# A two-layer decoder trunk with input and parameters laid out by feature, and its first four tiles made k-tile by k-tile

## The chip, the cores and the metric

The kernel runs on one core of a Trainium2 chip. The metric is the device time of one execution in microseconds. Before, the median of three runs is 1343.31 us.

## What is computed

A trunk of two layers on 512 tokens of width 1024, everything in float32. Each layer multiplies the normed input with one matrix of 3344 columns; its parts go to an attention with 8 heads and to a Mamba-2 state-space block (16 heads, a causal convolution of width 4 over x, B and C). Both outputs go through one output product into the residual, and a SwiGLU with a hidden width of 2816 follows.

```python
def hybrid_mixer(h, w_in, ...):
    proj = h @ w_in
    q, k, v, z, xbc, dt = jnp.split(proj, [Q_END, K_END, V_END, Z_END, XBC_END], axis=-1)
    attn = dilated_attention(q, k, v)                      # after a partial rotary on q and k
    xbc = jax.nn.silu(causal_depthwise_conv(xbc, conv_w, conv_b))
    dt = jax.nn.softplus(dt + dt_bias)
    y = ssd_chunked(xs, dt, -jnp.exp(a_log), bm, cm) + d_skip[:, None] * xs
    y = rmsnorm(y * jax.nn.silu(z), ssm_norm)              # in two groups
    return jnp.concatenate([attn, y], axis=-1) @ w_out

for layer in range(DEPTH):
    h = h + hybrid_mixer(rmsnorm(h, norm_mix[layer]), w_in[layer], ...)
    h = h + swiglu(rmsnorm(h, norm_ffn[layer]), w_gate[layer], w_up[layer], w_down[layer])
return rmsnorm(h, final_norm)
```

## The kernel before

The residual lies feature-major on the chip: eight tiles hT of 128 features by 512 tokens. A float32 product is made of three products in float32r: both operands are split into a high part and a low rest (xh, xl and whi, wlo), and hi x hi, hi x lo and lo x hi are added in one accumulator. One output tile of 128 columns over 8 k-tiles is thus 24 products of 512 columns (`block`, line 506). dt's tile needs only 16, since its 16 columns hold high and low parts side by side. The norm's scale (one number per token) is put on the accumulator as it is read out (`scaled`, line 744), so the products don't wait for it; but every read of an accumulator does wait for the norm's row.

The program is a list of operations, each with an engine, a duration and a priority (a due time, set by `at`). A list schedule (`Plan.schedule`, line 217) runs a model of the engines and takes, on each engine, the ready operation of the lowest priority number; the order that comes out is fixed, and every engine runs its instructions in that order. SyncE's DMA queue goes by priority alone and stops where a load waits for its buffer. PSUM has 3 buffers for accumulators (acc), 2 held longer (hold) and 3 for transposes and small things (tr); there are 2 buffers for raw weights of up to 2048 columns each and 3 each for whi and wlo; 56 buffers (G) hold 128 x 512 tiles.

The head of the program, which the change touches:

- Lines 446 to 457: ident (the identity for transposes), mrow (norm weights of the mixer as rows) and the first half of the input, token-major, are loaded. mrow is transposed to pmix (line 465).
- Line 575: the weights of the first two tiles, 128 columns each. The chunk for the third and fourth tile (line 765) waits for a raw buffer, and the loads behind it in the queue wait with it.
- Lines 577 to 588: each input tile is transposed on TensorE (4 transposes a tile, 32 in all) into PSUM; `split_x` takes xh (ScalarE) and xl (VectorE) from there, and a copy makes hT; its squares are summed for the norm.
- Lines 591 to 618: the other parameters arrive as rows (prow, crow) and are transposed to prm and cvp; lines 643 to 657 spread d_skip over features with a product (dskr, dsk). The constant array cst (line 605) feeds the selectors sele, lt, rt and, with the positions, the rotary tables (lines 661 to 735).
- Lines 763 to 774: the first two tiles of layer 0 are made in halves, since the second half of the input comes later; then tiles three and four. `conv` (line 753) reads a finished accumulator (tile cu, with the norm's row), and does one ScalarE step, three VectorE steps and a Silu. Behind these four tiles come dt's (line 779) and the tiles of x and z.

`Norm.spread` (line 557) makes the row: eight small products sum the squares over features (tr<-ones,sq), VectorE scales them (var), GpSimd raises them to -0.5 (rcol, line 554), four transposes and a ScalarE copy spread them to all partitions (rstd).

Of the kernel before, what the change touches and what calls it, by code (L numbers as in the profile page):

```python
# [13 lines left out]
I32 = mybir.dt.int32  # L14
# [5 lines left out]
P = 128  # L20
# [29 lines left out]
# columns of the constant array  # L50
# [3 lines left out]
# columns of the transposed parameter rows  # L54
PC_MIX, PC_FFN, PC_FIN, PC_SSM, PC_DTB, PC_ALOG, PC_DSK, PC_W = 0, 16, 32, 40, 64, 66, 68, 70
# [103 lines left out]
class VTile:  # L159
    """A tile that gets its place when its first operation is emitted."""  # L160
# [22 lines left out]
class Plan:  # L183
# [139 lines left out]
def hybrid_trunk(  # L323
    ctx: ExitStack,
    tc: tile.TileContext,
    x, positions, norm_mix, w_in, conv_w, conv_b, dt_bias, a_log, d_skip, ssm_norm,
    w_out, norm_ffn, w_gate, w_up, w_down, final_norm, consts, out,
# [43 lines left out]
    def at(t):  # L371
        plan.t = t

    # ---- operations
# [52 lines left out]
    def mms(outs, prods, each, prio=None):  # L427
        """prods: (out, lhsT, rhs, start, stop), or (out, in, identity) for a transpose."""
# [17 lines left out]
    at(-40.0)  # L446
    ident = C([P, P], "ident")
# [3 lines left out]
    xt = {}  # L451

    def load_x(hf):
        for i in range(NT):
            xt[i, hf] = G("x")
            load(xt[i, hf], x[0, i * P:(i + 1) * P, hf * S:(hf + 1) * S], 256)
    load_x(0)
# [5 lines left out]
    pmix = C([P, 16], "pmix")  # L463
    t = tr()
    tposes(t, [(t[:, 0:16], mrow, ident[0:16, 0:16])])
    copy("dve", pmix, t[:, 0:16])

# [1 line left out]
    # A chunk is one load; its pieces, 128 columns each, are split into float32r parts hi + lo.  # L469
# [36 lines left out]
    def block(segs, lead=LEAD, t=None, total=None, done=0):  # L506
        """One output tile: segs of (weight piece, operands, first and last k-tile)."""
        t = acc() if t is None else t
        total = total or sum(k1 - k0 for _, _, k0, k1 in segs)
        for pid, xl, k0, k1 in segs:  # L510
            at(clock[0] - lead)
            if whl[pid][4] is None:
                split_w(pid, "pool" if pid == 1 else "dve")
                whl[pid].append(k0)
# [16 lines left out]
    hT = [C([P, S], f"hT{k}") for k in range(KD)]  # L531

    class Norm:
        """Sum of squares over feature tiles, then 1/rms per token, as a row on all partitions."""
# [39 lines left out]
    # the first operands, out of the token-major input  # L574
    p_first = rows(w_in[0], 0, KD, XBC_COL + 1024, P) + rows(w_in[0], 0, KD, XBC_COL + 1024 + P, P)
    xs_next, norm_next = [], Norm(KD)
    for k in range(KD):
        if k == 4:
            at(-30.0)
            load_x(1)  # L580
        at(-20.0 + k)
        t = hold() if k < 2 else acc() if k == 2 else tr()
        tposes(t, [(t[:, i * P:(i + 1) * P], xt[i, k // 4][:, (k % 4) * P:(k % 4 + 1) * P], ident) for i in range(NT)])
        xs_next.append(split_x(t, pmix[:, k:k + 1]))
        at(-9.0 + k)
        copy("dve" if k % 2 else "act", hT[k], t)
        at(0.4 * k)
        norm_next.square(hT[k])
# [603 lines left out]
```

## Time and profile before

| | |
|---|---|
| runs, us | 1338.26, 1343.31, 1344.51 |
| median, us | 1343.31 |
| span of the profiled execution, us | 1336.7 |
| TensorE busy, us | 1310.3 (98%) |
| VectorE busy, us | 789.0 (59%) |
| ScalarE busy, us | 608.4 (46%) |
| GpSimd busy, us | 143.2 (11%) |
| DMA | 115.46 MB, 86 GB/s in the mean |

The span runs from the first to the last instruction of one execution under the profiler; a time of that execution apart from its span is not among the figures. PE is TensorE, PEld its weight loads, DVE VectorE, ACT ScalarE, POOL GpSimd, SP SyncE with the DMA queue. A matmul's busy time is modelled and overlaps the next one's, so the distance between two starts is what a product takes, not its duration. L436 and the like are lines of helpers, so the tile names tell what an instruction does.

### The profile page before, as it was taken

What the parts mean: (1) busy time and instruction counts of PE and PEld (TensorE: products, weight loads), DVE (VectorE), ACT (ScalarE), POOL (GpSimd) and SP (SyncE); (2) the same over time, 40 slices, a digit from 0 to 9 for tenths busy, and PEclk for the clock granted to TensorE, in tenths of its full rate; (3) what the DMA queues carried; (4) which work ended last, traced back from release to release, by engine and by line L of the source; (5) the groups of instructions that cost most, each with busy time, mean ns of one, the idle gap of its engine ahead of it and who ended that gap; (6) DMA issues with size and microseconds to landing.
All of it is one profiled execution on the core that took longest, in us unless ns stands there. A gap on an engine that the chain in (4) does not pass through costs nothing.

```text
span 1336.7 us, 15604 instructions
## 1 busy us (share of the span) xinstructions
PE 1310.3 (98%) x6118; PEld 1053.4 (79%) x6118; DVE 789.0 (59%) x1312; ACT 608.4 (46%) x956; POOL 143.2 (11%) x111
## 2 busy tenths in 40 slices
PE   7999998999999999999999999999999999999997
PEld 6778777678888888888888777767788888888876
DVE  5996689766444334444469687887744433344443
ACT  5878755654332223223347686466532222232233
POOL 1002456000000000000000235520000000000000
PEclk9999999999999999999999999999999999999999
DMA  5221111222222232222322221111332323332141
GB/s 176 95 95 64 63 63 32 64 63 95 95 95 75 96 129 95 95 87 96 117 84 76 67 92 64 38 58 38 91 115 84 97 74 102 111 123 67 61 160 63
DMA packets 111744, 115.46 MB, mean 86 GB/s; under 512 B 4492, under 2 KB 102072, under 8 KB 111672
## 3 DMA queue, kind: packets, MB, share of 16 engines
q1 hardware_dynamic: 111672, 114.47, 26.7%
q8 instruction: 48, 0.79, 0.3%
q14 instruction: 24, 0.20, 0.0%
HBM read 112.37 MB, written 2.10 MB: 86 GB/s over the span
## 4 chain that ended last, share of the span: by engine, by line
PE 89%; DVE 5%; ACT 2%; POOL 2%; issue 1%; DMA 1%; SPq 0%; POOLq 0%; DVEq 0%; ACTq 0%
PE acc L436 79%; PE tr L436 4%; PE tr L434 3%; PE hold L436 3%; DVE qs L384 1%; DVE xbc L395 1%; DVE wlo L384 1%; ACT whi L421 1%; POOL qr L384 0%; DMA raw<-in_w_down_dram 0%; POOL xbc L384 0%; DMA x<-in_x_dram 0%; DVE qs L949 0%; DVE sa L390 0%; DVE sa L1007 0%
## 5 line engine op out<-in xcount | busy, mean ns | idle before, releaser
L436 PE MATMUL acc<-xh,whi 128*128 128x512 f32 x1584 | 628.2, 397 | 1.4 <-ACT whi L421 1.1
L436 PE MATMUL acc<-xl,whi 128*128 128x512 f32 x1584 | 618.6, 391 | 0.0
L436 PE MATMUL acc<-xh,wlo 128*128 128x512 f32 x1568 | 613.2, 391 | 0.3 <-DVE wlo L384 0.3
L421 ACT CAST whi<-raw 128x1024 fp32r<-128x1024 f32 (+4 forms) x260 | 224.0, 867 | 490.3 <-PE acc L436 455.9
L436 PEld LDWEIGHTS acc<-xh,whi 128*128 128x128 f32 x1584 | 298.3, 188 | 66.8 <-issue 5.5
L436 PEld LDWEIGHTS acc<-xh,wlo 128*128 128x128 f32 x1568 | 295.0, 188 | 64.2 <-DVE wlo L384 1.5
L436 PEld LDWEIGHTS acc<-xl,whi 128*128 128x128 f32 x1584 | 298.5, 188 | 59.2 <-issue 0.5
L384 DVE TENSOR_TENSOR wlo<-raw,whi 128x1024 fp32r<-128x1024 f32 (+4 forms) x251 | 258.7, 1035 | 63.0 <-ACT whi L421 62.3
L384 DVE TENSOR_TENSOR ga<-acc,rstd 128x512 f32<-128x512 f32 x44 | 30.4, 692 | 182.4 <-PE acc L436 181.8
L384 DVE TENSOR_TENSOR hT<-hT,acc 128x512 f32<-128x512 f32 x80 | 54.8, 685 | 109.0 <-PE acc L436 108.3
L423 ACT ACT_TABLE_LOAD x54 | 69.3, 1283 | 6.4 <-DVE pmix L401 3.5
L555 POOL TENSOR_TENSOR rcol<-var,nhalf 128x4 f32<-128x4 f32 x8 | 8.7, 1091 | 558.3 <-DVE var L390 558.3
L395 DVE SCALAR_TENSOR_TENSOR xbc<-cu,cvp,xbc 128x511 f32<-128x511 f32 (+2 forms) x72 | 58.5, 816 | 3.2 <-ACT xbc L423 2.3
L384 DVE TENSOR_TENSOR up<-acc,rstd 128x512 f32<-128x512 f32 x44 | 30.3, 688 | 45.0 <-PE acc L436 44.9
L421 ACT CAST xh<-ga 128x512 fp32r<-128x512 f32 x44 | 27.4, 623 | 58.4 <-DVE ga L384 58.4
L423 ACT ACTIVATE sa<-sa,mx 128x512 f32<-128x512 f32 (+3 forms) x64 | 36.0, 562 | 36.6 <-DVE mx L1007 35.1
L1151 POOL TENSOR_TENSOR fr<-fvar,nhalf 128x1 f32<-128x1 f32 x4 | 2.2, 547 | 356.9 <-DVE fvar L390 356.9
L384 DVE TENSOR_TENSOR xl<-ga,xh 128x512 fp32r<-128x512 f32 x44 | 30.3, 688 | 15.1 <-ACT xh L421 15.1
L1007 DVE CUSTOM_DVE_ANT_0 sa<-tr,cst 128x512 f32<-128x512 f32 (+3 forms) x64 | 30.5, 477 | 10.3 <-PE tr L436 10.1
L384 DVE TENSOR_TENSOR ga<-ga,up 128x512 f32<-128x512 f32 x44 | 30.3, 689 | 3.7 <-ACT ga L423 1.4
L384 DVE TENSOR_TENSOR ee<-ee,cbm 128x512 f32<-128x512 f32 x32 | 26.0, 817 | 6.9 <-ACT ee L423 6.9
L384 POOL TENSOR_TENSOR xbc<-xbc,er 128x384 f32<-128x384 f32 x16 | 20.1, 1258 | 83.3 <-DVE er L384 43.1
(203 smaller groups left out, 1184.9 us busy)
## 6 DMA issues: line engine op xcount, KB each, us to landing
raw<-in_w_in_dram SPq DMA_DIRECT2D x25, 1024.0 KB, 5.0
raw<-in_w_gate_dram SPq DMA_DIRECT2D x20, 1024.0 KB, 5.2
raw<-in_w_up_dram SPq DMA_DIRECT2D x20, 1024.0 KB, 5.3
raw<-in_w_down_dram SPq DMA_DIRECT2D x16, 768.0 KB, 4.3
raw<-in_w_out_dram SPq DMA_DIRECT2D x8, 1024.0 KB, 4.9
raw<-in_w_down_dram SPq DMA_DIRECT2D x12, 640.0 KB, 4.4
raw<-in_w_out_dram SPq DMA_DIRECT2D x8, 512.0 KB, 5.0
x<-in_x_dram SPq DMA_DIRECT2D x8, 256.0 KB, 4.6
```

What stands on the lines that cost most here:

```text
L384: lambda: ENG[eng].tensor_tensor(R(o), R(a), R(b), alu))
L395: lambda: nc.vector.scalar_tensor_tensor(R(o), R(a), R(s), R(b), op0, op1))
L421: nc.scalar.copy(R(o), R(a))
L423: nc.scalar.activation(R(o), R(a), func, **kw)
L434: nc.tensor.transpose(R(p[0]), R(p[1]), R(p[2]))
L436: nc.tensor.matmul(R(p[0]), R(p[1]), R(p[2]), start=p[3], stop=p[4])
L555: lambda: nc.gpsimd.tensor_tensor(R(self.r), R(v), R(nhalf), ALU.pow))
L1007: nc.vector.tensor_tensor_reduce(R(sa[:, 0:nk]), R(t[:, 0:nk]), R(cst[:, C_MASK + S - nk:C_MASK + S]), 1.0, 3e38, ALU.add, ALU.min, R(m))
L1151: lambda r=r, v=v: nc.gpsimd.tensor_tensor(R(r), R(v), R(nhalf[:, 0:1]), ALU.pow))
```

## The change

The host hands over the input transposed (xT, feature by token), the positions by partition, and one array `columns` with all small parameters already as columns on 128 partitions (d_skip spread over features, dt_bias and a_log on the rows of the four quadrants). The loads put them in place: hT directly from xT, pmix, prm and posi from the arrays. All transposes of the input and of parameter rows are gone, as are mrow, prow, crow, cvp, posr and the product for d_skip. pmix is kept for the first split; every later use of the norm weights reads prm.

The first four output tiles of layer 0 are no longer made one after another with weights cut by `split_w`. Each k-tile's weights for all four, 128 x 512, are a load of their own (raw0, in G buffers); hT and weights of one k-tile are loaded in turn. For each k, xh, xl, wh and wl are made, and 12 products go to four accumulators that stay open through all 8 k-tiles: two acc and two hold.

```diff
-    load(ident, consts[:, C_ID:C_ID + P], 64)
-    mrow = C([16, P], "mrow")
-    load(mrow, norm_mix.rearrange("l (k p) -> (l k) p", p=P), 8)
...
+    pmix = C([P, 16], "pmix")
+    load(pmix, columns[:, PC_MIX:PC_MIX + 16], 8)
+    hT = [C([P, S], f"hT{k}") for k in range(KD)]
+    raw0 = []
+    for k in range(KD):
+        load(hT[k], xT[k * P:(k + 1) * P, :], 256)
+        raw0.append(G("w0"))
+        load(raw0[k], w_in[0, k * P:(k + 1) * P, XBC_COL + 1024:XBC_COL + 1024 + S], 256)
...
-    p_first = rows(w_in[0], 0, KD, XBC_COL + 1024, P) + rows(w_in[0], 0, KD, XBC_COL + 1024 + P, P)
+    first = [acc(), acc(), hold(), hold()]
     for k in range(KD):
-        if k == 4:
-            at(-30.0)
-            load_x(1)
         at(-20.0 + k)
-        t = hold() if k < 2 else acc() if k == 2 else tr()
-        tposes(t, [(t[:, i * P:(i + 1) * P], xt[i, k // 4][:, (k % 4) * P:(k % 4 + 1) * P], ident) for i in range(NT)])
-        xs_next.append(split_x(t, pmix[:, k:k + 1]))
-        at(-9.0 + k)
-        copy("dve" if k % 2 else "act", hT[k], t)
-        at(0.4 * k)
+        xs_next.append(split_x(hT[k], pmix[:, k:k + 1]))
+        wh, wl = split_x(raw0[k], None)
+        for j, t in enumerate(first):
+            js = slice(j * P, (j + 1) * P)
+            xh, xl = xs_next[k]
+            mms([t], [(t, wh[:, js], xh, k == 0, False), (t, wh[:, js], xl, False, False),
+                      (t, wl[:, js], xh, False, k == KD - 1)], 0.2165, clock[0])
+            clock[0] += 3 * 0.2165
+        at(-12.0 + k)
         norm_next.square(hT[k])
...
     at(-12.0)
-    prow = C([PC_W, P], "prow")
...
+    prm = C([P, PC_W], "prm")
+    load(prm, columns, 94)
+    posi = C([P, NT], "posi", I32)
+    load(posi, positions, 2)
+    ident = C([P, P], "ident")
+    load(ident, consts[:, C_ID:C_ID + P], 64)
     cst = C([P, C_W], "cst")
     load(cst, consts, 400)
...
-            first = [block([(pb[i], xs, 0, 4)], 24.0, None, KD) for i in range(2)]
-            for i in range(2):
-                xbc[8 + i] = conv(block([(pb[i], xs, 4, KD)], 24.0, first[i], KD, 4), 8 + i)
+            for i in range(4):
+                xbc[8 + i] = conv(first[i], 8 + i)
...
-                    stt(xbc[jj], xbc[jj], dsk[:, l * 8 + jj:l * 8 + jj + 1], yd[u2], ALU.mult, ALU.add)
+                    stt(xbc[jj], xbc[jj], pcol(PC_DSK + l * 8 + jj), yd[u2], ALU.mult, ALU.add)
```

With the four tiles made ahead of `layer`, the due time at which layer 0 starts (T0), and with it that of the norm's row and of the four convolutions, is 20.8 where it was 0. The bytes loaded for the head are the same: 2 MB of input and 2 MB of weights for the four tiles.

## Rows read from the trace of the kernel before

**Rows 1.** The page's busy table, whole span.

```profile
PE 1310.3 (98%) x6118; PEld 1053.4 (79%) x6118; DVE 789.0 (59%) x1312; ACT 608.4 (46%) x956; POOL 143.2 (11%) x111
```

**Rows 2.** Stretches: length, busy us (instructions), granted clock, DMA share, GB/s.

```profile
0.00:10.00 10.00, 4.03 (x15) 3.08 (x16) 1.16 (x3) 2.23 (x3) 2.41 (x10) 1.00 0.74 218
10.00:20.00 10.00, 9.23 (x41) 6.97 (x40) 8.04 (x12) 9.34 (x15) 2.39 (x1) 1.00 0.74 242
...
60.00:80.00 20.00, 20.00 (x91) 16.06 (x89) 19.36 (x35) 12.55 (x17) 0.00 (x0) 1.00 0.18 59
```

**Rows 3.** TensorE in order of time, head: start, duration, instruction, idle before.

```profile
4.09 0.48 PE L434 MATMUL hold<-ident,x 128*128 128x128 f32 x1 [0.90 <-DMA x<-in_x_dram]
5.96 0.48 PE L434 MATMUL hold<-ident,x 128*128 128x128 f32 x1 [1.40 <-DMA x<-in_x_dram]
...
11.41 0.79 PE L436 MATMUL acc<-xh,whi 128*128 128x512 f32 x1 [0.73 <-ACT whi L421]
...
14.12 0.63 PE L436 MATMUL acc<-xh,wlo 128*128 128x512 f32 x1
14.54 1.88 PE L434 MATMUL tr<-ident,x 128*128 128x128 f32 x12
```

**Rows 4.** Chain that ended last, 15 to 30 us: start, length, what.

```profile
19.63 8.21 PE acc L436 x36
```

**Rows 5.** TensorE and VectorE in order of time, 27 to 43 us.

```profile
27.68 0.95 PE L436 MATMUL tr<-ones,sq 128*128 128x1 f32 x8
...
31.36 1.29 DVE L384 TENSOR_TENSOR cu<-acc,rstd 128x512 f32<-128x512 f32 x2 [2.09 <-ACT rstd L421]
...
39.73 0.47 PE L436 MATMUL acc<-xh,whi 128*128 128x512 f32 x1 [0.27 <-DVE pairsel L637]
...
42.21 0.39 PE L436 MATMUL tr<-dskr,halfsel 16*128 16x16 f32 x2
```

**Rows 6.** SyncE's DMA issues in order of time.

```profile
1.64 1.83 SPq L440 DMA_DIRECT2D x<-in_x_dram  x4
...
17.97 0.36 SPq L440 DMA_DIRECT2D cst<-in_consts_dram  x1
```

**Rows 7.** Groups by shape, whole span: count, busy us, mean ns, idle before.

```profile
L384 DVE TENSOR_TENSOR wlo<-raw,whi 128x1024 fp32r<-128x1024 f32 x139 | 171.7, 1236 | 24.6 <-ACT whi L421 24.1
...
L423 ACT ACT_TABLE_LOAD x54 | 69.3, 1283 | 6.4 <-DVE pmix L401 3.5 <-DVE xbc L395 2.1
...
L384 DVE TENSOR_TENSOR wlo<-raw,whi 128x512 fp32r<-128x512 f32 x48 | 35.3, 735 | 1.4 <-ACT whi L421 1.4
...
L421 ACT CAST whi<-raw 128x512 fp32r<-128x512 f32 x48 | 29.5, 618 | 24.3 <-PE acc L436 19.0 <-issue 3.9 <-ACT sa L423 1.0
...
L395 DVE SCALAR_TENSOR_TENSOR xbc<-cu,cvp,xbc 128x511 f32<-128x511 f32 x24 | 19.4, 808 | 2.5 <-ACT xbc L423 2.3
L423 ACT ACTIVATE sq<-hT 128x512 f32<-128x512 f32 x32 | 19.3, 621 | 0.0
...
L395 DVE SCALAR_TENSOR_TENSOR xl<-hT,prm,xh 128x512 fp32r<-128x512 f32 x16 | 11.9, 746 | 0.4 <-ACT xh L423 0.4
...
L423 ACT ACTIVATE xh<-hT,prm 128x512 fp32r<-128x512 f32 x16 | 11.5, 718 | 1.7 <-DVE hT L384 1.7
```

**Rows 8.** Stretch 31 to 56 us, rotary tiles alone: VectorE, ScalarE busy, then clock.

```profile
31.00:56.00 25.00, 4.33 (x31) 0.46 (x2) 1.00 0.31 102
```

**Rows 9.** GpSimd's power op of each layer's second norm, layer 1's first dt product.

```profile
319.40 1.01 POOL L555 TENSOR_TENSOR rcol<-var,nhalf 128x4 f32<-128x4 f32 x1 [88.37 <-DVE var L390]
...
693.65 0.39 PE L436 MATMUL acc<-xh,whi 128*128 128x512 f32 x1
...
972.01 1.01 POOL L555 TENSOR_TENSOR rcol<-var,nhalf 128x4 f32<-128x4 f32 x1 [88.39 <-DVE var L390]
```

**Rows 10.** Stretches late in layer 0's mixer, columns as in rows 2.

```profile
210.00:220.00 10.00, 7.75 (x38) 6.26 (x37) 9.28 (x14) 5.11 (x11) 8.25 (x6) 1.00 0.34 105
220.00:230.00 10.00, 8.51 (x35) 6.19 (x35) 9.82 (x21) 6.67 (x14) 5.99 (x5) 0.83 0.00 0
```

More of the change, by code (lines that the diff above doesn't have):

```diff
@@ L81, in _constants, with _columns, put @@
     c[:, C_INVF:C_INVF + HROPE] = 500000.0 ** (-np.arange(0, ROPE, 2) / ROPE)
+    return c
+def _columns(inputs):
+    c = np.zeros((P, PC_W), np.float32)
+    def put(c0, name):
+        a = np.asarray(inputs[name]).reshape(-1, P)
+        c[:, c0:c0 + a.shape[0]] = a.T
+    put(PC_MIX, "norm_mix")
+    put(PC_FFN, "norm_ffn")
+    put(PC_SSM, "ssm_norm")
+    put(PC_CB, "conv_b")
+    put(PC_CW, "conv_w")
+    for c0, name in ((PC_DTB, "dt_bias"), (PC_ALOG, "a_log")):
+        for q in range(4):
+            c[q * 32:q * 32 + NH, c0:c0 + DEPTH] = np.asarray(inputs[name]).T
+    c[:, PC_DSK:PC_DSK + 8 * DEPTH] = np.repeat(np.asarray(inputs["d_skip"]), 64, axis=1).reshape(-1, P).T
     return c
@@ L325, in hybrid_trunk @@
     tc: tile.TileContext,
-    x, positions, norm_mix, w_in, conv_w, conv_b, dt_bias, a_log, d_skip, ssm_norm,
-    w_out, norm_ffn, w_gate, w_up, w_down, final_norm, consts, out,
+    xT, positions, w_in, w_out, w_gate, w_up, w_down, final_norm, consts, columns, out,
 ):
@@ L588, in hybrid_trunk @@
         norm_next.square(hT[k])
     at(-12.0)
-    prow = C([PC_W, P], "prow")
-    memset("pool", prow, 0.0)
-    for src, r, nr in ((norm_ffn, PC_FFN, 16), (ssm_norm, PC_SSM, 16)):
-        load(prow[r:r + nr, :], src.rearrange("l (k p) -> (l k) p", p=P), 8)
-    for src, r in ((dt_bias, PC_DTB), (a_log, PC_ALOG), (d_skip, PC_DSK)):
-        load(prow[r:r + 2, 0:NH], src, 1)
-    crow = C([120, P], "crow")
-    load(crow[0:24, :], conv_b.rearrange("l (t p) -> (l t) p", p=P), 12)
-    load(crow[24:120, :], conv_w.rearrange("l w (t p) -> (l w t) p", p=P), 48)
@@ L601, in hybrid_trunk @@
-    posi = C([NT, P], "posi", I32)
-    load(posi, positions.rearrange("o (i p) -> (o i) p", p=P), 2)
-    at(-1.0)
+    prm = C([P, PC_W], "prm")
[4 more added lines that the diff above has]
+    load(ident, consts[:, C_ID:C_ID + P], 64)
     cst = C([P, C_W], "cst")
     load(cst, consts, 400)
-    at(1.0)
-    cvp = C([P, 120], "cvp")
-    t = tr()
-    tposes(t, [(t[:, 0:120], crow, ident[0:120, 0:120])])
-    copy("act", cvp, t[:, 0:120])
@@ L612, in hybrid_trunk @@
-    at(6.0)
-    for q in range(1, 4):
-        copy("dve", prow[64:PC_W, q * 32:q * 32 + NH], prow[64:PC_W, 0:NH])
-    prm = C([P, PC_W], "prm")
-    t = tr()
-    tposes(t, [(t[:, 0:PC_W], prow, ident[0:PC_W, 0:PC_W])])
-    copy("act", prm, t[:, 0:PC_W])
     tri = cst[:, C_TRI:C_TRI + P]
     def conv_wcol(l, w, j):
-        c = 24 + (l * 4 + w) * NCONV + j
-        return cvp[:, c:c + 1]
+        return pcol(PC_CW + (l * 4 + w) * NCONV + j)
     def conv_bcol(l, j):
-        return cvp[:, l * NCONV + j:l * NCONV + j + 1]
+        return pcol(PC_CB + l * NCONV + j)
@@ L628, in pcol @@
     def pcol(c):
-        return pmix[:, c:c + 1] if c < 16 else prm[:, c:c + 1]
+        return prm[:, c:c + 1]
     at(8.0)
@@ L1180 @@
     arrays, args = {}, []
-    for name in _INS + ['consts']:
-        a = _constants() if name == 'consts' else np.ascontiguousarray(inputs[name])
+    data = {"xT": np.ascontiguousarray(np.asarray(inputs["x"])[0].T),
+            "positions": np.ascontiguousarray(np.asarray(inputs["positions"]).reshape(NT, P).T)}
+    data.update((name, np.ascontiguousarray(inputs[name])) for name in _INS)
+    data.update(consts=_constants(), columns=_columns(inputs))
+    for name in ["xT", "positions"] + _INS + ["consts", "columns"]:
+        a = data[name]
         arrays[f"in_{name}_dram"] = a
```

47 lines of the change are left out of this document (6 added, 41 removed).

## Prediction

> **What bounds the kernel now.** I read the busy table first: TensorE is busy 1310.3 us of a 1336.7 us span [rows 1], so 26.4 us of idle time is all that an edit can take out, unless it takes work off TensorE or raises its clock. Second, the table by stretches, to see where that idle time lies: in the first 10 us TensorE is busy only 4.03, in the next 10 it idles 0.77 more; the 20 us from 60 on have no idle time, while VectorE is busy 19.36 of 20 there [rows 2]. So the head waits for operands, and the stage behind it runs two engines full at once. Third, TensorE in order of time: the first transpose of the input starts at 4.09, a later one waits for its load until 5.96, and the first product starts only at 11.41 [rows 3]. Around 14.12 to 14.54 work follows at a distance of 0.42 us for 512 columns, which is the lower clock level, 1.2 GHz; later 36 products take 8.21 us on the chain of waits, 0.228 each, the upper level, 2.4 GHz [rows 3, 4]. The clock column says 1.00 for the whole head [rows 2], so there the distance between products is what tells the level. The four first tiles take 96 products; the next tile (dt) has its first product at 39.73 [rows 5]. All behind that point is the same work in both kernels, so the question is when TensorE gets there, and whether the other engines can follow.
>
> **The new head, step by step.** On SyncE's queue pmix now takes the place of ident, hT0 that of mrow, and the first weight tile that of the first input tile (issue at 1.64; four issues take 1.83, so 0.46 each [rows 6]). A first 256 KB tile landed 4.09 - 1.64 = 2.45 us after its issue [rows 3, 6]; hT0, issued 0.46 earlier, lands at about 3.6. The second tile before, issued at 2.1, landed at 5.96; the weight tile, one place earlier, lands at about 5.5, with bounds of 4.1 (as quick as a first one) and 6.0. ScalarE then has a table load (1283 ns), xh (718 ns) and wh (618 ns) [rows 7]. Table and xh fit between 3.6 and 5.6; wh ends at 6.2, or at 6.9 if the planner puts the first square (621 ns, [rows 7]) ahead of it. I take 6.7 for the first product, bounds 5.3 and 8.0.
>
> From then on supply must keep up. One k-tile is 12 products: 12 x 0.228 = 2.7 us of TensorE at the upper level, 5.1 at the lower. For it ScalarE does xh, wh and a square, 718 + 618 + 621 ns = 1.96 us; VectorE does xl, wl and a sum, 746 + 735 ns and no more than wl's 735 again, 2.2 us [rows 7]. The loads are 512 KB per k-tile; the DMA engines moved 242 GB/s at a busy share of 0.74 between 10 and 20 us [rows 2], so 327 at full share and 1.6 us. All three are below 2.7, so I expect no gaps between k-tiles.
>
> How long the clock stays low is not shown for this order. Before, it rose 3.1 us after the first product (11.41 to 14.54) and 10.4 us after the first transpose [rows 3]. A microsecond at the low level does the work of 0.228 / 0.427 = 0.53 us, so it costs 0.47: bounds 1.5 and 4.9 us. I take 5 us at the low level, nearer to the first row because the products come without a break: 2.3.
>
> So the 96 products end at 6.7 + 96 x 0.228 + 2.3 = 30.9. The column sums of the norm follow (eight, 0.95 by their row [rows 5]; I take 0.8, since the end of one product lies beside the next) and the row's four transposes (a third of the 12 that took 1.88 [rows 3], 0.6): dt's work stands where it stood at 39.73 by 32.3. That is 7.4 us. The 32 input transposes (12 of them from 14.54 on, [rows 3]) and those of the parameter rows are in it, since they lie before 39.73; the d_skip products at 42.21, 0.3 to the next product [rows 5], come on top: 7.7 us.
>
> **What rides along at no cost on the path.** VectorE loses copies of hT, prow, halfsel and dskr, ScalarE those of hT, cvp and prm. In their place the weights of the first four tiles are split in 8 pieces of 512 columns, not 4 of 1024, under the products of the first 30 us; each is counted in the supply above. The constant array's load moves from 17.97 [rows 6] to behind the 17 first loads, whose issues take 17 x 0.46 = 8 us; if the queue fills up it comes later, by 13 to 17 us, still before it is needed at the row. So selectors and rotary tables are made before the norm's row, not behind it. pmix, positions and parameters come as 128 short rows each; only pmix gates anything, and hT0's landing covers it. A pmix one microsecond later than hT0 costs that microsecond, which is in the bound of 8.0.
>
> **What gets tighter.** The norm's row now comes behind all 96 products. Before, the sums at 27.68 gave scaled tiles from 31.36 on [rows 5], 3.7 us later. Now the sums start at 30.9, the first accumulator is free by 30.9 + 3.7 + 0.65 = 35.3, while dt (16 products, 3.6 us) keeps TensorE until 35.9. It fits with 0.6 us to spare; cost 0 to 1, I take 0.2. Then four convolutions come at once: 4 x (0.65 + 3 x 0.8) = 12.2 us of VectorE in a lump [rows 5, 7], ahead of dt's chain and of the scaled copies that free accumulators for the next tiles. TensorE is 7.5 us ahead and the row 3 us later, so VectorE must make up some 10 us. Rotary steps of 4.33 us (31 of them between 31 and 56 us, [rows 8]) move ahead of the row, and so do three weight splits of 1.24 [rows 7], since raw and split buffers are free earlier: 8.0. The rest, about 2 us, is an unpaid lump, and I let VectorE's idle time behind 80 us take it. Layer 1 is a control without a head: from dt's first product at 693.65 to the power op of the next norm it needs 972.01 - 693.65 = 278.4 us, layer 0 needs 319.40 - 39.73 = 279.7 [rows 5, 9]. Layer 0 is thus only 1.3 us worse than an undisturbed one, 0.3 of it d_skip. I count this stretch as unchanged.
>
> Sum: 7.7 - 0.2 = 7.5 us off a span of 1336.7, so 1329.2. The three runs are 1338.26 to 1344.51; 1.6 to 7.8 us lie around this span, 6.6 at the median of 1343.31. The forecast is **1335.8**.
>
> **A rule against this order.** Between loads each k-tile has 2.7 us of products against 1.6 us of loading, as worked out above. The Trainium skill, TensorE: Matmul & The Clock Gate, section HAM oscillation, warns of just such a k-outer loop: the products of one k-tile, then a wait for the next load, in which the clock falls back, again at every k-tile. It advises finishing all k-tiles of one output first. By that rule the slower rival (d) would happen; the rows speak against its condition here.
>
> **The rivals.**
> (a) VectorE's lump isn't paid: accumulators come free late around the third and fourth tile behind dt, or the state-space chain reaches the mixer's end late. For it: 19.36 of 20 [rows 2], and between 210 and 230 us TensorE idles 2.25 + 1.49 us already and the clock dips to 0.83 [rows 10]. Against: layer 1. Price: 2 to 7 us given back, 1338 to 1343; most likely 1341.
> (b) The new order falls better: constants out of the crowd, so those 3.7 us and the dip shrink. Gain 10 to 12: 1331 to 1333.
> (c) The low level lasts as long as in the long bound (2.5 more) and the first product starts at 8.0 (1.3 more): 1339.6.
> (d) The clock doesn't rise in the first four tiles, because every k-tile comes later than the products of the one before end: 96 x 0.427 = 41.0 us instead of 21.9 + 2.3, 16.8 more than forecast: 1352.6. It decides where the low level lasts longer than (7.5 + 2.3) / 0.47 = 21 us; from there the kernel is slower than before. Against: 1.6 to 2.2 us of supply for 2.7 us of products.
> (e) The head doesn't start earlier, since ScalarE's first steps wait for something not seen here: 1343.
>
> **How the numbers follow.** Forecast 0.52 (its own range 1332 to 1340), (a) 0.21, (b) 0.12, (c) 0.07, (d) 0.05, (e) 0.03. A range for 8 in 10 takes in (b), (c) and about half of (a), and widens the lower end for runs that lie as close to the span as the quickest: 1329 to 1342. About 0.5% (6.7 us, so below 1336.6) is what a measurement of this kernel can tell from no change. The forecast is 0.8 us beyond that line, so I put 0.36 of its 0.52 there; with (b) faster 0.48. Slower: (d) and 0.02 of (a), 0.07. Same: 0.45.
>
> **What would show it.** First product between 5.3 and 8.0; products 0.43 us apart for 3 to 7 us, then 0.228 without gaps to about 31; the sums there, the first scaled tile 3.7 us later; no wait for an accumulator before 60 us; 278 to 281 us from dt's first product to the next norm's power op. Gaps between k-tiles, sums long before the last of the 96 products, or over 284 us in that stretch would make the forecast wrong.

## The result and the profile after

The changed kernel takes 1329.82 us in the median of six runs (1329.59 to 1332.83); the kernel before, run beside it, 1342.41 (1337.47 to 1344.69). The ratio is 0.9924, with a 95% interval of 0.9903 to 0.9945. The forecast was 1335.8. The profiled execution has a span of 1328.1 us and a time of 1329.88; the span of before was 1336.7. So 8.6 us of span are gone where 7.5 were expected, and the medians lie 12.6 us apart. Where the other 4 us come from is a question for the experiments. One later run of the changed kernel took 1859.75 us at a granted clock of 0.655 and is left out of every comparison.

The page's busy table of the changed kernel. Beside [rows 1], TensorE has 7.9 us less busy time in 38 fewer instructions (36 transposes and the two products for d_skip), VectorE 3.0 less, ScalarE 9.2 less.

```profile
PE 1302.4 (98%) x6080; PEld 1048.7 (79%) x6080; DVE 786.0 (59%) x1302; ACT 599.2 (45%) x949; POOL 139.4 (10%) x109
```

The same stretches as in [rows 2] and, from 200 us on, those that answer to [rows 10] (length, busy us of PE, PEld, DVE, ACT and POOL, granted clock, DMA share, GB/s):

```profile
0.00:10.00 10.00, 2.98 (x7) 2.38 (x8) 3.75 (x6) 6.06 (x10) 2.26 (x9) 1.00 0.80 265
10.00:20.00 10.00, 10.00 (x43) 8.21 (x43) 9.95 (x19) 10.00 (x21) 0.00 (x0) 1.00 1.01 324
...
200.00:210.00 10.00, 7.76 (x37) 6.29 (x36) 9.28 (x16) 4.81 (x9) 8.55 (x6) 0.95 0.30 107
210.00:220.00 10.00, 9.33 (x34) 6.93 (x34) 9.69 (x21) 6.53 (x15) 5.23 (x5) 0.71 0.00 0
```

Between 10 and 20 us everything is full at once: TensorE, VectorE and ScalarE busy 9.95 to 10 of 10, the DMA engines at a share of 1.01. Supply runs ahead of the products: VectorE's last split of a first weight tile ends at 18.38, and the products of that k-tile start at 28.02. Behind 200 us TensorE idles 2.24 + 0.67 us, and the clock dips deeper than before (0.95 and 0.71 here, 1.00 and 0.83 in [rows 10]).

The head of TensorE in order of time (start, duration, instruction, and in brackets the idle time before it), against [rows 3, 5]:

```profile
7.02 0.80 PE L454 MATMUL acc<-xh,xh 128*128 128x512 f32 x1 [7.02 <-ACT xh L439]
...
10.60 0.58 PE L454 MATMUL hold<-xh,xl 128*128 128x512 f32 x1
11.02 0.39 PE L454 MATMUL hold<-xh,xh 128*128 128x512 f32 x1
11.25 0.39 PE L454 MATMUL hold<-xl,xh 128*128 128x512 f32 x1
...
30.75 0.95 PE L454 MATMUL tr<-ones,sq 128*128 128x1 f32 x8
31.55 1.07 PE L452 MATMUL tr<-ident,ropetok 128*128 128x128 f32 x8
32.38 0.48 PE L454 MATMUL acc<-xh,whi 128*128 128x512 f32 x1
```

Products stand 0.43 apart until 11.02, then 0.23 without a break until the column sums at 30.75. The rotary tables' transposes follow, and dt's first product comes at 32.38 where it came at 39.73 [rows 5]. ScalarE shows why the first product isn't earlier than 7.02: the table load begins only when hT0 has landed, and the first square stands between xh and the weights' high part (here also named xh, read from w). ScalarE in order of time:

```profile
3.93 1.28 ACT L441 ACT_TABLE_LOAD   x1 [3.93 <-DMA hT<-in_xT_dram]
5.22 0.72 ACT L441 ACTIVATE xh<-hT,pmix 128x512 fp32r<-128x512 f32 x1
5.85 0.61 ACT L441 ACTIVATE sq<-hT 128x512 f32<-128x512 f32 x1
6.37 0.60 ACT L439 CAST xh<-w 128x512 fp32r<-128x512 f32 x1
```

SyncE's issues: the constants' load goes out at 12.19 where it went at 17.97 [rows 6].

```profile
12.19 0.33 SPq L458 DMA_DIRECT2D cst<-in_consts_dram  x1
```

VectorE's first scaled tile in the changed kernel, 3.9 us behind the sums ([rows 5]: 3.7), without any accumulator wait on TensorE before 60 us:

```profile
34.65 1.29 DVE L402 TENSOR_TENSOR cu<-acc,rstd 128x512 f32<-128x512 f32 x2 [2.75 <-ACT rstd L439]
```

GpSimd's power operations serve as milestones, since each ends a norm: here the norm's row, the last norm of layer 0's mixer (called **G** from here on) and the feed-forward norm (**F**; 319.40 in [rows 9]), each with its idle time before:

```profile
32.04 1.02 POOL L565 TENSOR_TENSOR rcol<-var,nhalf 128x4 f32<-128x4 f32 x1 [29.26 <-DVE var L408]
...
212.91 1.02 POOL L565 TENSOR_TENSOR rcol<-var,nhalf 128x4 f32<-128x4 f32 x1 [2.94 <-DVE var L408]
309.81 1.01 POOL L565 TENSOR_TENSOR rcol<-var,nhalf 128x4 f32<-128x4 f32 x1 [88.33 <-DVE var L408]
```

In the profile of before G is at 222.60. So 9.69 us are won at G and 9.59 at F; 8.6 are left at the end, and the table below shows where the last one goes.

### The profile page after: what moved, and what is told of

Same layout as the page of the kernel before. It is cut to its first block, busy times and chain, and to the rows that moved or that the text cites. A ratio compares the mean times of both kernels' runs of the same rounds, so it can differ in the third digit from the quotient of the medians.

```text
span 1328.1 us, 15509 instructions
## 1 busy us (share of the span) xinstructions
PE 1302.4 (98%) x6080; PEld 1048.7 (79%) x6080; DVE 786.0 (59%) x1302; ACT 599.2 (45%) x949; POOL 139.4 (10%) x109
## 4 chain that ended last, share of the span: by engine, by line
PE 88%; DVE 6%; ACT 2%; POOL 2%; issue 1%; DMA 1%; POOLq 0%; SPq 0%; ACTq 0%; DVEq 0%
PE acc L454 78%; PE tr L454 4%; PE hold L454 4%; PE tr L452 3%; DVE wlo L402 1%; DVE qs L402 1%; POOL xbc L402 1%; DVE xbc L413 1%; POOL qr L402 1%; DMA raw<-in_w_down_dram 0%; ACT whi L439 0%; DVE qs L913 0%; DVE qr L402 0%; ACT L441 0%; DVE sa L408 0%
## 5 line engine op out<-in xcount | busy, mean ns | idle before, releaser
L454 PE MATMUL acc<-xh,whi 128*128 128x512 f32 x1552 | 614.5, 396 | 0.5 <-ACT whi L439 0.4
L454 PE MATMUL acc<-xl,whi 128*128 128x512 f32 x1552 | 605.8, 390 | 0.0
L454 PE MATMUL acc<-xh,wlo 128*128 128x512 f32 x1536 | 599.9, 391 | 0.3 <-DVE wlo L402 0.3
L439 ACT CAST whi<-raw 128x1024 fp32r<-128x1024 f32 (+4 forms) x256 | 219.6, 864 | 496.3 <-PE acc L454 462.9
L454 PEld LDWEIGHTS acc<-xh,whi 128*128 128x128 f32 x1552 | 292.0, 188 | 63.9 <-issue 5.4
L454 PEld LDWEIGHTS acc<-xl,whi 128*128 128x128 f32 x1552 | 292.2, 188 | 57.9 <-issue 0.5
L454 PEld LDWEIGHTS acc<-xh,wlo 128*128 128x128 f32 x1536 | 288.9, 188 | 62.0 <-DVE wlo L402 0.7
L402 DVE TENSOR_TENSOR wlo<-raw,whi 128x1024 fp32r<-128x1024 f32 (+2 forms) x248 | 256.3, 1038 | 61.7 <-ACT whi L439 60.8
L413 DVE SCALAR_TENSOR_TENSOR xbc<-cu,prm,xbc 128x511 f32<-128x511 f32 (+2 forms) x72 | 58.3, 817 | 2.6 <-ACT xbc L441 1.9
```

The source lines that it names most:

```text
L402: lambda: ENG[eng].tensor_tensor(R(o), R(a), R(b), alu))
L413: lambda: nc.vector.scalar_tensor_tensor(R(o), R(a), R(s), R(b), op0, op1))
L439: nc.scalar.copy(R(o), R(a))
L454: nc.tensor.matmul(R(p[0]), R(p[1]), R(p[2]), start=p[3], stop=p[4])
```

## Experiments

Nine variants of the changed kernel were run, and three times one of the two kernels unaltered. None of them leaves work out; the warm-up products, the early copy and the additional loads in some of them feed no output. The table gives one profile of each: G, the two mixers' ends (from G to F, in layer 0 and in layer 1), the span and the median of the runs (a single run for the second and third profile of before and for the slow supply).

| kernel | first product | G | end, layer 0 | end, layer 1 | span | runs, us |
|---|---|---|---|---|---|---|
| before | 11.41 | 222.60 | 96.80 | 96.80 | 1336.7 | 1342.41 |
| before, second profile | 12.04 | 222.45 | 96.49 | 96.78 | 1336.2 | 1338.03 |
| before, third profile | 12.26 | 222.57 | 99.54 | 99.49 | 1342.0 | 1343.82 |
| changed | 7.02 | 212.91 | 96.90 | 96.44 | 1328.1 | 1329.82 |
| changed, second profile | 7.65 | 214.61 | 96.44 | 96.74 | 1328.1 | 1330.51 |
| tiles in order | 7.19 | 220.48 | 96.91 | 99.23 | 1336.9 | 1337.96 |
| layout alone | 10.51 | 217.75 | 99.53 | 99.22 | 1336.0 | 1334.08 |
| k-tile order alone | 11.53 | 219.36 | 96.44 | 96.75 | 1333.2 | 1338.37 |
| constants late | 7.04 | 221.83 | 96.90 | 96.44 | 1336.7 | 1336.75 |
| row early | 7.03 | 214.58 | 97.19 | 99.63 | 1331.8 | 1332.95 |
| warm-up products | 7.12 | 211.44 | 96.74 | 96.70 | 1325.0 | 1329.08 |
| table early | 5.62 | 211.99 | 96.45 | 96.44 | 1324.9 | 1328.05 |
| both | 5.61 | 210.28 | 99.54 | 96.75 | 1329.4 | 1330.25 |
| slow supply | 7.13 | 228.89 | 96.43 | 96.72 | 1341.7 | 1343.75 |

Each mixer's end takes one of two values, 96.4 to 97.2 or 99.2 to 99.6, in every kernel. What remains, the span less G and less the two ends, is 919.5 to 922.8 in all fourteen. Most of that spread is one more place of this kind, in layer 1 between the mixer's first norm and its last: 75.6 to 75.7 us in eleven profiles, 77.1 to 77.2 in three (changed, constants late, both). There the granted clock of the changed kernel's first profile is 0.87 between 790 and 800 us, and in its second 1.00; this takes the 1.5 us that are won at F and missing at the end. So G is where the edits of the head can be compared, to some 2 us: the changed kernel's own two profiles differ by 1.7 there.

### Before, profiled again: what is the change's own?

> The kernel before, unaltered, one more profile: its runs lie at 1337 to 1338.5 with a mean granted clock of 0.995, or at 1342 to 1345 with 0.990 to 0.993. Theory: if the profile falls among the latter, the head is as in the first profile within 0.5 us (dt's first product at 39.7), and the additional time lies between 200 and 250 us and between 850 and 900 us, where the products' idle time at the mixers' ends is followed by a longer stretch at the low level: 2 to 3 us at each, 5 to 7 together. Rival: the additional time is in the first 40 us, where the clock rises later. If the profile falls among the quicker runs, its checkpoints repeat within 0.5 us.

> The kernel before once more, for a second chance at a profile of its longer runs; the expectations are those of the run ahead of it: additional time at 200 to 250 and 850 to 900 us (theory) or in the first 40 us (rival), or a repeat of the first profile within 0.5 us.

The first repeated the profile (222.45, 318.94). The second was a longer run, 1343.82 us at a mean clock of 0.990, and the theory held: its dt tile (39.75) and G stand where they stood, and both of its mixers' ends are 2.7 us longer, 5.4 of the 5.3 that its span has more. Stretches of that third profile of before (columns as above); [rows 10] has 0.83 where the first line has 0.52:

```profile
220.00:230.00 10.00, 8.27 (x24) 5.82 (x23) 9.36 (x20) 4.44 (x9) 5.56 (x5) 0.52 0.00 0
880.00:890.00 10.00, 9.32 (x36) 7.29 (x35) 7.75 (x15) 6.14 (x12) 5.64 (x4) 0.70 0.00 1
```

and TensorE in order of time behind G, same profile:

```profile
223.94 1.11 PE L434 MATMUL tr<-ident,rcol 128*128 128x128 f32 x4 [1.06 <-POOL rcol L555]
225.73 0.79 PE L436 MATMUL tr<-kh,qs 128*128 128x512 f32 x1 [0.68 <-ACT rstd L421]
226.32 0.63 PE L436 MATMUL tr<-kl,qs 128*128 128x512 f32 x1
...
230.59 0.42 PE L436 MATMUL acc<-xl,whi 128*128 128x512 f32 x1
230.85 0.40 PE L436 MATMUL acc<-xh,wlo 128*128 128x512 f32 x1
```

The same stretch in the first profile of before:

```profile
223.97 0.65 PE L434 MATMUL tr<-ident,rcol 128*128 128x128 f32 x4 [0.82 <-POOL rcol L555]
...
225.63 0.39 PE L436 MATMUL tr<-kl,qs 128*128 128x512 f32 x1
225.86 0.39 PE L436 MATMUL acc<-xh,whi 128*128 128x512 f32 x1
```

TensorE's starts agree to 0.03 us up to 220.0 in the two profiles. Then the clock falls a little later in the longer run, whose products are 0.28 us ahead by 221.8, so that its pause ahead of the transposes at 223.9 is 1.06 us and not 0.82. Behind it products are still 0.43 apart until 230; in the first profile they are 0.23 apart from 225.6 on. Of all 52 runs of before, 26 lie over 1342 and 21 under 1339. The median of a few runs therefore moves by some 5 us with how many of them had long ends.

### The changed kernel again

> The changed kernel unaltered, on the same chip as the run beside it. Theory (8.6 us of span are the change's, the rest of the 12.6 us between the two medians lies in how long the clock stays low at the ends of the mixers in the runs of the kernel before): its quickest runs again at 1329.6 to 1330, 8 to 8.5 us under the quickest of the kernel before, its slower ones at 1332 to 1335 with a granted clock of 0.992 to 0.993; power operation of layer 0's feed-forward norm within 0.5 us of 309.8. Rival (the change also steadies the clock, so that all 12.6 us are its own): no run of it over 1333.

The runs compared are 1328.75 to 1332.86, the ratio is 0.9919, with an interval of 0.9893 to 0.9946. The head of this profile is later than in the first. TensorE in order of time:

```profile
13.36 0.62 PE L454 MATMUL acc<-xl,xh 128*128 128x512 f32 x1
13.79 0.43 PE L454 MATMUL acc<-xh,xl 128*128 128x512 f32 x1
```

The first product comes at 7.65 and products are 0.43 apart until 13.79, so 6.1 us at the low level, not 4.0; the sums come at 32.45 and G at 214.61, 1.7 later (0.63 for the start, 2.1 x 0.47 = 1.0 for the level). F came at 311.05, 1.2 off its mark. Both expectations missed in part: no run went over 1333, as the rival had it, but the spread of 4.1 us is there. At G the change is thus worth 9.7 or 8.0 us by the two profiles; the quickest run against the quickest gives 1337.37 - 1328.75 = 8.6. I take 8 to 10 us as shown to be the change's own. It may also make the long ends rarer: 20 of the 52 runs of before lie at least 5.4 us above its quickest, which is what two long ends cost, and none of the changed kernel's eleven lies more than 4.1 above. Nothing was tried that would show a cause for this, so whether the rest of the 12.6 us is the change's stays open.

### The order undone, the layout kept

```diff
-        wh, wl = split_x(raw0[k], None)
-        for j, t in enumerate(first):
-            js = slice(j * P, (j + 1) * P)
+        ws0.append(split_x(raw0[k], None))
...
+    for j, t in enumerate(first):
+        js = slice(j * P, (j + 1) * P)
+        for k in range(KD):
...
+            wh, wl = ws0[k]
...
+            if prev is not None:
+                after_op(plan.ops[-1], prev)
+            prev = plan.ops[-1]
```

> The changed kernel with the first four tiles' products in tile order on TensorE (all 8 k-tiles of tile 0, then tile 1, ...); loads and splits stay in k-tile order, so only the order of the 96 products is undone. Theory A (the k-tile order is what lets TensorE use each k-tile as it arrives): tile 0 is paced by supply, its last product comes when the eighth k-tile is split, at about 18.4 us as in the changed kernel; 72 products of the other tiles and 16 of dt follow, 88 x 0.228 = 20 us, so these are done by about 40 us where the changed kernel has them at 37: 3 to 5 us longer in the span (1331 to 1333), more if the gaps keep the clock at the lower level. Rival B (the gain is only the missing transposes and the early start; the order doesn't matter, the planner fills gaps with other work): within 1 us of 1328.1.

The median is 1337.96 (ratio 0.9972, 0.9955 to 0.9988); G is 7.6 us later than in the changed kernel, more than the 3 to 5 expected; of the span's 8.8, 2.8 lie in a long end of layer 1. TensorE in order of time of this kernel:

```profile
12.94 0.50 PE L454 MATMUL acc<-xh,xl 128*128 128x512 f32 x1 [0.58 <-DVE xl L402]
...
24.93 0.79 PE L454 MATMUL acc<-xh,whi 128*128 128x512 f32 x1 [1.49 <-DVE whi L402]
25.52 0.63 PE L454 MATMUL acc<-xl,whi 128*128 128x512 f32 x1
```

A k-tile gives the first tile three products, 0.68 us of work, and comes every 1.4 to 1.5 us; the 24 products take from 7.19 to 18.93, where 24 in the changed kernel take from 7.02 to 14.43. Behind a later wait of 1.49 the clock is low, and products are 0.43 apart until 28.08. So the head without the k-tile order loses twice, to waits and to the level that follows them.

### Layout alone, and k-tile order alone

The layout alone:

```diff
-        raw0.append(G("w0"))
-        load(raw0[k], w_in[0, k * P:(k + 1) * P, XBC_COL + 1024:XBC_COL + 1024 + S], 256)
...
-    first = [acc(), acc(), hold(), hold()]
+    p_first = rows(w_in[0], 0, KD, XBC_COL + 1024, P) + rows(w_in[0], 0, KD, XBC_COL + 1024 + P, P)
...
+            first = [block([(pb[i], xs, 0, 4)], 24.0, None, KD) for i in range(2)]
+            for i in range(2):
+                xbc[8 + i] = conv(block([(pb[i], xs, 4, KD)], 24.0, first[i], KD, 4), 8 + i)
```

The k-tile order alone (the host hands over the input token-major here; the parameters still come as columns):

```diff
-        load(hT[k], xT[k * P:(k + 1) * P, :], 256)
...
+            load(xt[i, hf], xT[i * P:(i + 1) * P, hf * S:(hf + 1) * S], 256)
...
-        xs_next.append(split_x(hT[k], pmix[:, k:k + 1]))
+        t = tr()
+        tposes(t, [(t[:, i * P:(i + 1) * P], xt[i, k // 4][:, (k % 4) * P:(k % 4 + 1) * P], ident) for i in range(NT)])
+        xs_next.append(split_x(t, pmix[:, k:k + 1]))
+        copy("dve" if k % 2 else "act", hT[k], t)
```

> The layout part alone: input and parameters feature-major and loaded into place, but the first four tiles made as in the kernel before (weights in chunks of 128 columns by 8 k-tiles, the first two tiles in halves), constants behind the third weight chunk as before. Theory A: the first product must still wait for a whole weight chunk behind four input tiles, so it starts at about 10 us (11.41 before, 7.02 in the changed kernel); no transposes lie between the products; dt's products start at about 35.5, so the span falls by 4 to 5 us against before (to about 1332) and stays 3 to 4 above the changed kernel. Rival B (layout is all of it): within 1 us of 1328.1. Rival C (k-tile order is all of it): within 1 us of 1336.7.

> The k-tile order alone: the input comes token-major and is transposed on TensorE (32 transposes) as before, copies make hT; parameters come as columns; the four tiles are made k-tile by k-tile. Theory A: first product at about 9.5 to 10, since four input tiles and a weight tile must land and 16 transposes go ahead; the other 16 transposes (0.14 us each, 2.2) lie between the products; dt at about 36.8; span about 1333.5, 3 below before and 5 above the changed kernel. Rival B (order is all): 1328 to 1329. Rival C (layout is all): 1336.

The layout alone has a median of 1334.08 (ratio 0.9949, 0.9928 to 0.9969) and its G 4.85 us earlier than before; the order alone 1338.37 (0.997, 0.995 to 0.9991), 3.24 us earlier. Their sum of 8.1 lies between the 8.0 and the 9.7 that the changed kernel wins at G in its two profiles, so it isn't shown that the two do more together than apart. Both first products came later than expected, at 10.51 and 11.53. The profile of the layout alone fell on two long ends, so its span says less than its G. The span of the order alone is 1333.2, expected 1333.5; this profile is one of four quicker runs (1334.5 to 1335), the other six lie at 1338.0 to 1341.83.

### What the early constants are worth

```diff
+    const_ops = [o for o in plan.ops[n_const:] if o.eng in ("act", "dve", "pe")]
...
         norm.spread()
+        if l == 0:
+            w_ = norm.row.tile.writer
+            for o in const_ops:
+                o.deps.add(w_)
+                w_.users.append(o)
```

The work on the constants (selectors, rotary tables) is ordered behind the norm's row; their loads stay.

> The changed kernel with the work on the constants (selectors on ScalarE, rotary tables on VectorE, ScalarE and TensorE) put behind the norm's row in every engine's order; loads and head stay. Theory A (what makes the stretch from dt to the next norm 277.4 us long instead of 279.7 before is that this work left the crowd behind the row): 4.3 us of VectorE and some 8 us of ScalarE come back into that crowd, the stretch grows to 279 to 281 and the span to 1330 to 1331.5, the head stays at 32.4. Rival B (that stretch is bound by TensorE alone and the 2.2 us come from the transposes of the rotary tables and the d_skip products that moved or went): the stretch grows by at most 1 us, the 0.8 of the rotary transposes that come back into it, span within 0.8 of 1328.1.

The first product is at 7.04, as in the changed kernel, but the low level lasts longer, until 12.75, and the sums come 0.96 later. G comes at 221.83: 8.9 us later, so some 8 us of it behind the head. The span is 1336.7, where theory A had 1330 to 1331.5, and the median 1336.75 (0.997, 0.9952 to 0.9988). TensorE in order of time of this kernel:

```profile
31.71 0.94 PE L454 MATMUL tr<-ones,sq 128*128 128x1 f32 x8
...
65.15 0.50 PE L454 MATMUL acc<-xh,whi 128*128 128x512 f32 x1 [2.26 <-DVE cu L402]
65.48 0.39 PE L454 MATMUL acc<-xl,whi 128*128 128x512 f32 x1
```

Accumulators come free late, 3.22 us of idle time between 60 and 100 us and 2.93 between 100 and 150 (0.22 and 0.95 in the changed kernel). This is the prediction's rival (a), made to happen.

### The norm's row early

```diff
         T0 = clock[0]
+        at(T0 if l else 0.0)
+        norm.spread()
         at(T0)
-        norm.spread()
```

> The changed kernel with the norm's row of layer 0 due at once: its column sums go on TensorE as soon as the eight squares are summed (about 21.4 us) and not behind all 96 products. The first scaled tile then waits for its accumulator alone, about 31.3 us where the changed kernel has 34.65. Theory A (that lump is paid already; with early constants TensorE never waits for VectorE between 31 and 100 us): the span stays within 1 us of 1328.1. Rival B (the late row still costs in the mixer): 1325 to 1327.

The row's power operation came at 25.15, not 32.04, and G at 214.58: 1.7 later than in the changed kernel's first profile, with 1.97 us of idle time between 100 and 150 us. The median is 1332.95 (0.9932, 0.9907 to 0.9957). The span of 1331.8 isn't within theory A's 1 us of 1328.1, mostly by its later G and a long end in layer 1 (99.63); but it is later and not earlier, so an early row wins nothing.

### Two edits that add to the gain at G

The warm-up products:

```diff
+    t = tr()
+    mms([t], [(t[:, 0:P], ones, ones, True, True)] * 13, 0.4)
```

The early table, with the first weight split ahead of the first square:

```diff
+    act(warm, ones[:, 0:1], AF.Copy, scale=ones[:, 1:2])
...
+        if k == 0:
+            after_op(hT[0].tile.readers[-1], wh.tile.writer)
```

> The changed kernel with 13 products of a constant tile (128 columns, result unused) on TensorE ahead of the first product, while it waits for its first operands. Theory A (the 4.0 us at 0.43 us spacing from 7.02 to 11.02 are the clock at its lower level after idleness): the first real products follow at 0.228 already, about 9 of them each 0.2 us earlier, the sums come at about 28.9, span 1326.3. Rival B (the low spacing has another cause, such as operands that come late): the first nine products keep their 0.43 and the span stays at 1328.1. If the 13 products take longer than 7 us, the first real product is late by the difference.

> The changed kernel with a one-column scaled copy on ScalarE at the very start, so that the activation table is loaded before the first input tile lands, and with the first weight tile's high part ahead of the first square. Theory A (the first product at 7.02 hangs on ScalarE: table load 3.93 to 5.21, xh, a square of 0.5, then wh): xh starts at 3.95, wh follows as soon as its tile has landed (5.0 to 5.8), first product at 5.7 to 6.4, span 0.6 to 1.3 us less, 1326.8 to 1327.5. Rival B (the weight tile lands only just before 6.4): first product at 7.0, nothing gained.

TensorE in order of time with the warm-up products (the 13 stand in the trace as 26 instructions):

```profile
0.99 4.59 PE L454 MATMUL tr<-ones 128*128 128x128 f32 x26 [0.99 <-POOL nhalf L422]
7.12 0.50 PE L454 MATMUL acc<-xh,xh 128*128 128x512 f32 x1 [1.54 <-ACT xh L439]
...
8.18 0.39 PE L454 MATMUL acc<-xh,xh 128*128 128x512 f32 x1
8.41 0.39 PE L454 MATMUL acc<-xl,xh 128*128 128x512 f32 x1
```

ScalarE in order of time with the early table:

```profile
0.73 1.28 ACT L441 ACT_TABLE_LOAD   x1 [0.73 <-PEq L1152]
...
4.14 0.72 ACT L441 ACTIVATE xh<-hT,pmix 128x512 fp32r<-128x512 f32 x1 [1.82 <-DMA hT<-in_xT_dram]
4.95 0.62 ACT L439 CAST xh<-w 128x512 fp32r<-128x512 f32 x1
```

With the warm-up the products are 0.23 apart from the first few on, the sums come at 29.26 (28.9 expected), and F comes 1.63 earlier than in the changed kernel's first profile; with the table early the first product comes at 5.62, F 1.37 earlier (low level for 5.3 us). Theory A held for both; the spans, 1325.0 and 1324.9, are 1.3 and 1.9 us better than it had. The medians are 1329.08 (0.9906, 0.9879 to 0.9933) and 1328.05 (0.9902, 0.9878 to 0.9926).

> The changed kernel with both edits of the two runs before: a small scaled copy on ScalarE at the start brings the activation table in early and the first weight split stands ahead of the first square; ten ones-by-ones products on TensorE run before the first product. Theory (the two gains add, because one is the first product's start and the other the clock level behind it): first product at about 5.6, products 0.23 us apart from the first three or four on, last of the 96 at about 27.7, the power operation of layer 0's feed-forward norm at 306.7 to 307.4 (309.81 in the changed kernel, 308.18 and 308.44 with one edit each), a span of 1323 to 1324 where layer 1 has its short stretches of low clock, and a median of 1325 to 1328. Rival (the supply becomes the bound: ScalarE's 1.96 us and the loads of each k-tile now stand against products at 2.7 us from the first k-tile on): gaps of 0.3 us and more between the first k-tiles, last of the 96 at about 28.8 as in the better of the two, the power operation at 308 or later, no gain over either alone.

TensorE in order of time with both edits (the early table and ten warm-up products):

```profile
27.91 0.95 PE L454 MATMUL tr<-ones,sq 128*128 128x1 f32 x8
```

GpSimd's G and F in the same kernel:

```profile
210.28 1.31 POOL L570 TENSOR_TENSOR rcol<-var,nhalf 128x4 f32<-128x4 f32 x1 [2.93 <-DVE var L408]
309.82 1.01 POOL L570 TENSOR_TENSOR rcol<-var,nhalf 128x4 f32<-128x4 f32 x1 [91.11 <-DVE var L408]
```

Up to G the theory held: sums at 27.91, G 2.63 earlier than in the changed kernel's first profile (1.47 and 0.92 for one edit each, so they add as far as one profile of each can tell). Then the end of layer 0's mixer was a long one, and F is where it was without any edit. Against the expectation of 1325 to 1328 the runs gave 1330.25 (1327.85 to 1331.53; ratio 0.9914, 0.9893 to 0.9935), beside 1330.51 for the changed kernel. The rival, a bound by the supply, isn't seen either: the products run without a wait from 6.83 on. What is won at G isn't shown in the runs: no version is shown to beat the changed kernel.

### A slower supply

```diff
         load(raw0[k], ...)
+        for n_ in range(4):
+            load(G("spare"), xT[k * P:(k + 1) * P, :], 256)
```

> The changed kernel with four extra loads of 256 KB behind each k-tile's two, into spare buffers that nothing reads: 1.5 MB per k-tile, about 4.85 us at 324 GB/s, against 2.73 us of products at the upper clock level and 5.1 at the lower. This makes the condition of the rival in which every k-tile comes later than the products before it end. Theory A (gaps of 2.1 us per k-tile leave the clock at the upper level once it has risen): products of 0.228 in each k-tile, last of the 96 at about 43. Rival D (the clock stays or falls back to the lower level in this order): products 0.43 apart in most k-tiles, last of the 96 at about 48. What follows is late in both, since the constants come behind these loads: the span is 20 us or more above 1328.

TensorE in order of time of this kernel:

```profile
26.74 0.50 PE L454 MATMUL acc<-xh,xh 128*128 128x512 f32 x1 [0.54 <-ACT xh L439]
...
30.90 0.50 PE L454 MATMUL acc<-xh,xh 128*128 128x512 f32 x1 [0.63 <-ACT xh L439]
...
38.83 0.39 PE L454 MATMUL hold<-xh,xl 128*128 128x512 f32 x1
...
43.49 0.50 PE L454 MATMUL acc<-xh,whi 128*128 128x512 f32 x1 [3.83 <-DVE whi L402]
...
45.02 0.63 PE L454 MATMUL acc<-xh,whi 128*128 128x512 f32 x1
45.45 0.63 PE L454 MATMUL acc<-xl,whi 128*128 128x512 f32 x1
```

The DMA engines moved more than the 324 GB/s of the expectation (387 between 20 and 30 us), so k-tiles come about every 4.1 us and not 4.85. TensorE waits 0.5 to 0.6 us at each (and 0.23 more inside), but between the waits the products stay 0.23 apart: the clock doesn't fall, as in theory A, with shorter waits than its 2.1 us. The last of the 96 starts at 38.83, and the span is 13.6 us longer than the changed kernel's, not 20. The clock falls once, at 45.0, behind a wait of 3.83 us. The Trainium skill, TensorE: Matmul & The Clock Gate, section HAM oscillation, warns of a loop over k-tiles in which the wait for the next load is longer than a k-tile's products, so that each k-tile starts at the low level. Here the waits are shorter than the products, and the run doesn't show it; longer ones at every k-tile weren't tried.

## Why the prediction was right, and where not

The result lies 6.0 us under the forecast and within its range, near the lower end. The mechanism was right; the size of one term was not.

- **First product**: 7.02, forecast 6.7. hT0 gave ScalarE its start at 3.93, forecast 3.6; the square did come ahead of the weights' split, a case that the prediction named.
- **Low level**: 4.0 us in one profile, 6.1 in another, forecast 5; the loss of 0.47 for each microsecond held between the two.
- **End of the 96**: sums at 30.75, forecast 30.9; no gaps between k-tiles. dt's first product at 32.38, forecast 32.3. That this came out to 0.15 us is in part luck, since the late start and the shorter low level of this profile cancel; in the second profile the sums come at 32.45.
- **The row's lateness**: the first scaled tile came 3.9 us behind the sums, forecast 3.7, and cost nothing.
- **The stretch from dt to the feed-forward norm**: 309.81 - 32.38 = 277.4 us, forecast 278 to 281 and "unchanged" from 279.7. Of the 2.2 us (279.67 to 277.43), 0.8 are the rotary tables' transposes, which moved ahead of dt (31.55 to 32.38), 0.3 is d_skip's product, and 0.6 is idle time of TensorE (5.92 us in this stretch before, 5.29 after); the row's transposes inside dt take 0.4 back. The rest, some 0.9, is what the clock gives in sum: one dip is gone, the one around G is deeper in this profile. The dip is seen in the stretch that holds the mixer's first gated norm. Before:

```profile
140.00:150.00 10.00, 9.00 (x46) 6.65 (x45) 6.80 (x10) 8.35 (x12) 4.51 (x4) 0.83 0.32 105
```

After:

```profile
130.00:140.00 10.00, 9.37 (x56) 7.06 (x55) 5.96 (x9) 5.83 (x10) 4.59 (x4) 1.00 0.33 105
140.00:150.00 10.00, 9.79 (x45) 6.80 (x44) 10.00 (x13) 7.57 (x10) 6.69 (x5) 1.00 0.00 0
```

  A mean of 0.83 over 10 us is 3.4 us at half speed, at 0.47 each 1.6 us. All three profiles of before have this dip, and neither of the changed kernel's. It is a small part of rival (b). Of the 3.7 us of idle time that (b) names around G, 2.9 are left, but with the deeper dip nothing comes of it: the end behind G takes 96.90 after 96.80.
- **The term that was mis-sized** is the last one, the 6.6 us between span and median. Outside the span lie only 1.7 to 2.2 us in every run (1329.88 - 1328.1, 1338.03 - 1336.2, 1343.82 - 1342.0). The rest of the 6.6 was no overhead: the profiled run of before had two short ends, the run at its median was longer. The sum from 1336.7 to 1329.2 came within 1.1 of the span of 1328.1; adding 1.7 would have given 1330.9. The prediction had widened its range downwards for runs that lie as close to the span as the quickest, and this is what held.
- **The lump on VectorE** was rightly called paid, but its stake was too small. The prediction had 4.33 us of rotary steps and three weight splits pay for it, and priced its failure at 2 to 7 us; with the constants' work behind the row 8.9 us were lost at G, some 8 of them behind the head.
- **Rivals (c), (d) and (e)** did not decide it. The second profile went some way towards (c), with 7.65 and 6.1 us; its span is 1328.1 all the same, since layer 0's end is 0.5 us quicker and the place in layer 1 that has two values 1.5 us. (d) did not come with waits of 0.5 to 0.6 us at every k-tile.

## What to carry to other kernels

When a head is short of operands, load so that the first arrivals give the most work: with four accumulators open each k-tile carries 2.7 us of products instead of 0.7, and the layout change without that gave about half of the gain at G. Ask also what can be done on the other engines while the head runs, because work that fits in there can be worth more than its own length once the next stage is crowded: here 4.3 us of VectorE's work (with some of ScalarE's), put back into the crowd, cost about 8. Compare edits at a milestone ahead of the places where the clock may stay low for a short or a long time, and split a median into its span and the granted clock of its runs before using the difference as a constant.

## What the hardware showed

- The same program keeps the low clock level around the mixer's last norm for some 3 us or for 10 (before, behind 220 us), and the mixer's end takes 96.4 to 97.2 or 99.2 to 99.6 us with it. TensorE's starts agree to 0.03 us until the clock falls. What decides between the two stays open; nothing was tried that separates it.
- The granted clock column reads 1.00 over the first 10 us although the products there stand 0.43 apart; in the head only their distance tells the level.
- A wait of 1.49 us in the kernel with tiles in order was followed by 3.2 us at the low level, while waits of 0.5 to 0.6 every 4.1 us with the slow supply were not, nor was the one of 1.54 between the warm-up products and the first product, nor one of 2.26 with the constants late (products 0.23 apart from 65.48 on). The length of one wait does not decide it.
- The activation table's load takes its place on ScalarE only when the operand of the first activation has landed (3.93), though it needs nothing of it; an earlier small activation moves it to 0.73. The next activation starts 1.29 us after the load does, here and at 43 of the changed kernel's 49 loads. The Trainium skill, ScalarE: Activation LUTs, section What ACT_TABLE_LOAD costs, adds a drain of about as much again for a switch to another set; no run here shows one.
- The DMA engines moved 387 GB/s between 20 and 30 us with the slow supply, at a share of 1.05, against 324 at 1.01 in the changed kernel.
- How long the low level lasts in the head differs from run to run, in both kernels. In the third profile of before the first product comes 0.85 us later than in the first (12.26 for 11.41), but products are then 0.23 apart, where the first profile has 0.43 until 14.5 [rows 3]; G is at 222.57 and 222.60. In the changed kernel, 0.63 us of a later first product and 2.1 us more at the low level went the same way and came out as 1.7 us at G. The third profile of before, TensorE in order of time:

```profile
13.86 0.40 PE L436 MATMUL acc<-xh,whi 128*128 128x512 f32 x1
14.10 0.39 PE L436 MATMUL acc<-xl,whi 128*128 128x512 f32 x1
```
